# Output stage of a gated two-mixer decoder block: who adds, when the gates are multiplied, in what order the weights come

## The chip, the cores and the metric

The kernel runs on one core of a Trainium2 chip. The metric is the device time of one execution in microseconds (us). TensorE (PE) multiplies matrices into PSUM; VectorE (DVE), ScalarE (ACT) and GpSimd (POOL) work element by element; SyncE (SP) issues the DMAs.

## The reference, cut to what matters

One block on x of shape (1, 1024, 1024), all in float32:

```python
h = rmsnorm(x, mix_norm_g)
qa, ka, va, q_lat, kv_lat, k_r, g_a, g_b = split(h @ w_in)
o_a = sliding_window_attention(rope(qa), rope(ka), va, sinks)     # 8 heads of 64
o_b = latent_attention(q_lat, kv_lat, k_r)                        # 8 heads, causal
y = sigmoid(g_a) * (o_a @ w_o_swa) + sigmoid(g_b) * (o_b @ w_o_mla)
x = x + y @ w_out
h = rmsnorm(x, ffn_norm_g)
x = x + (silu(h @ w_gate) * (h @ w_up)) @ w_down
return rmsnorm(x, final_norm_g)
```

w_o_swa and w_o_mla are 512 x 1024, w_out is 1024 x 1024. The change lies in the line of y and in what leads up to it.

## The kernel before, in words

**Products.** Every float32 operand is split into a high part (a cast by ACT, L163) and a low part (a subtraction by DVE, L166); `split` (L161) does both. `mm3` (L168) makes one product out of three matmuls, high x high (L172), high x low (L173) and low x high (L174). Weights are loaded by `st.load_to` (the DMA is L238) into a raw tile `wr` and split by `st.conv_to`, in the order in which `plain` has listed them.

**Stages around the change.** First the projections and the sliding-window attention are done; o_a lies transposed in HBM (`oa_d`), the gates lie in HBM too (`gate_d`). Then comes the loop over the latent attention (L1353 to 1393): 64 tiles t = 8 heads x 8 blocks of 128 queries. One tile's turn issues the scores of tile t + 2 (L1171: matmuls L1182 to 1184 into `scb`, maximum on DVE, exp on ACT L1193, normalization on POOL), the pv products that have come due (L1213, matmuls L1231 and 1232 into `ob`), and the transposes of tile t (L1198: L1209 into `pTb`, split into `pth` and `ptl`).

**What is woven into the attention.** PE has the product o_a x w_o_swa as filling: `mix_a` (L1270) computes, for an output chunk dc of 128 columns and a half sh of 512 rows, 12 matmuls of 128x512 into `oA`, in halves of 6 at the tiles listed in `slots` (L1348), and copies the result with ACT (L1286) to `ar`; for dc below 4 that goes to HBM (`ar_d`) and comes back later. `units` (L1347) are the first 24 halves, `rest` (L1394) the four whole units left over. o_a itself is loaded by `load_oa` (L1249, tile `oar`) and split by `split_oa` (L1253). `load_q` and `load_k` fetch the next heads' queries and keys.

**The output stage** (L1400 to 1444): eight output chunks dc in the order `DCS` (L1304). For each, `load_sigs` (L1306) has fetched the two gates (tiles `sg`) and for dc below 4 `ar`; `sigmoids` (L1418) applies the sigmoid on ACT, a chunk ahead; `mix_b` (L1400) first lets POOL multiply `ar` with gate a (L1407, two halves), then for each half makes 12 matmuls o_b x w_o_mla into `oB` and lets DVE multiply the PSUM tile with gate b (L1412), then for each half adds the two (L1415 through `add`, L180: DVE for the first half, POOL for the second, except in the last chunk) and splits y into `yh` and `yl`, the operand of the next product. There are four PSUM banks for `oB` (psum_phase("psc", 4)). After the stage the product y x w_out runs (L1615, `xo`): for each block of 128 rows one sum over eight k = dc.

**What sets the order.** From L1039 to L1593 a scheduler orders the instructions of each engine out of the program by estimates; the order is not written out by hand. What runs through `tc.keep_in_program_order` (the casts of `split` while `held[0]` is set, L160 to 165) stays in its place. Each engine then runs its instructions in order. SP issues the DMAs in order too, and a DMA whose tile is not free holds up those behind it. Big tiles come from two pools of slots, U (21 of 128x1024) and V (17 of double size).

Of the kernel before, what the change touches and what calls it, by code (L numbers as in the profile page):

```python
# [89 lines left out]
def hybrid_block_kernel(  # L90
# [65 lines left out]
    def PX(name, shape=(P, 512)):  # L156
        return psum["x"].tile(list(shape), F32, tag="ps", name=uid(name))
# [10 lines left out]
    def mm3(ps, pairs, first=True, last=True, go_on=False):  # L168

        n = len(pairs)  # L170
        for i, ((ah, al), (bh, bl)) in enumerate(pairs):
            nc.tensor.matmul(ps, ah, bh, start=first and i == 0, stop=False, skip_group_check=go_on)  # L172
            nc.tensor.matmul(ps, ah, bl, start=False, stop=False, skip_group_check=go_on)  # L173
            nc.tensor.matmul(ps, al, bh, start=False, stop=last and i == n - 1, skip_group_check=go_on)  # L174
# [4 lines left out]
    def add(out, a, b, eng):  # L179
        eng.tensor_tensor(out, a, b, op=ALU.add)  # L180
# [4 lines left out]
    def half(s):  # L185
        return slice(512 * s, 512 * s + 512)
# [47 lines left out]
    def plain(key, src, shape, wide=False, k0=None):  # L234

        def load():
            raw = U("wr", F32, shape)
            nc.sync.dma_start(raw, src)  # L238
            return raw

        def conv(raw):
            hi, lo = halves_of(shape, wide)
            if k0 is None:
                split(hi, lo, raw)
            else:
                split_g(hi, lo, raw, k0)
            return hi, lo

        st.add(key, load, conv)
# [50 lines left out]
        plain(("oa", dp), w_o_swa[dp], (P, 4, 256), True)  # L300
    for dp in (2, 0, 3, 1):
        plain(("ob", dp), w_o_mla[dp], (P, 4, 256))
    for r, hf in enumerate((0, 1, 0)):
        for j in range(4):
            plain(("out", r, j), w_out[hf, j], (P, 2, 512), (r, j) != (2, 3))


# [945 lines left out]
    def split_oa(g, sh, c):  # L1253
        raw, (hi, lo) = oa_raw[(g, sh)] if c == 0 else oa_raw.pop((g, sh))
        split(hi[:, c], lo[:, c], raw[:, c])
        oaT[(2 * g + c, sh)] = (hi[:, c], lo[:, c])
# [5 lines left out]
        nc.sync.dma_start(gate[i], gate_d[i])  # L1262

    def sigmoid(i):
        nc.scalar.activation(gate[i], gate[i], AF.Sigmoid)

    ar = {}
    oa_ps = {}
# [25 lines left out]
    def split_ob(c, sh):  # L1294
        if sh == 0:
            ob_hl[c] = hi_lo("obT")
        hi, lo = ob_hl[c]
        src = ob.pop(c) if sh else ob[c]
        split(hi[:, half(sh)], lo[:, half(sh)], src[:, half(sh)])
        obT[(c, sh)] = (hi[:, half(sh)], lo[:, half(sh)])  # L1300

    wo = {}
    NT = NH * NB
    DCS = (4, 5, 0, 6, 1, 2, 3, 7)  # L1304

    def load_sigs(dc):  # L1306
        for i in (dc, 8 + dc):
            load_sig(i)
        if dc < 4:
            ar[dc] = U("ar")  # L1310
            nc.sync.dma_start(ar[dc], ar_d[dc])
# [32 lines left out]
    load_k(2)  # L1344
    first = {0: (2, 0), 1: (2, 1), 2: (3, 0), 3: (3, 1)}
    fill = {}
    units = [(u // 2, u % 2, c) for u in range(16 - 4) for c in (0, 2)]  # L1347
    slots = [5, 6] + [NB * h + n for h in range(1, NH) for n in (1, 2, 5)] + [NT - 2]  # L1348
    for t, u in zip(slots, units):
        fill[t] = u  # L1350
    w_at = {t: u[0] // 2 for t, u in fill.items() if u[0] % 2 == 0 and u[1:] == (0, 0)}
# [1 line left out]
    for t in range(NT):  # L1353
        h, n = divmod(t, NB)
        if t + 2 < NT:
            scores(t + 2)
        while pvq and pvq[0][0] <= t:
            pv(*pvq.pop(0)[1:])
        if n == 2 and h + 2 < NH:
            load_q(h + 2)  # L1360
        if n == 6 and h + 3 < NH:
            load_k(h + 3)
        hh, nn = step(t)
        if nn % 2 == 1:
            pvq.append((t + 3, hh, nn // 2))
        e = t - (NT - 8)
        if e == 6:
            psum_phase("psc", 4)
        if t in first:
            prod_k(*first[t])  # L1370
        if t in fill:
            dc, sh, c0 = fill[t]
            mix_a(dc, sh, c0, 2, P1("oA") if c0 == 0 else None)
        transposes(t)
        held[0] = True
        if t == 0:
            load_oa(0, 1)
            load_oa(1, 1)
        if t < 8:
            split_oa(t % 4 // 2, t // 4, t % 2)  # L1380
        if t + 6 in w_at or t == 0:
            st.load_to(st.index[("oa", w_at.get(t + 6, 0))])
        if t + 2 in w_at:
            st.conv_to(st.index[("oa", w_at[t + 2])])
        if e == 4:
            load_sigs(DCS[0])
        if -3 <= e < 3:
            split_ob((e + 3) // 2, (e + 3) % 2)
        if e in (2, 6):
            st.load_to(st.index[("ob", 2 if e == 2 else 0)])  # L1390
        if e == 6:
            st.conv_to(st.index[("ob", 2)])
        held[0] = False
    rest = [(i // 2, i % 2) for i in range(12, 16)]  # L1394
    mix_a(*rest.pop(0), 0, 4, PX("oA"))
    for _, hp, j in pvq:
        pv(hp, j)
# [2 lines left out]
    def mix_b(dc, i):  # L1400
        if dc % 2 == 0:
            wo[4 + dc // 2] = st.get(("ob", dc // 2))
        w = wo[4 + dc // 2]
        ga, gb = gate.pop(dc), gate.pop(8 + dc)
        a_ = ar.pop(dc)
        for sh in range(2):
            nc.gpsimd.tensor_tensor(ga[:, half(sh)], a_[:, half(sh)], ga[:, half(sh)], op=ALU.mult)  # L1407
        for sh in range(2):
            cs = half(sh)
            pb = PX("oB")  # L1410
            mm3(pb, [((w[0][:, c, blk(dc % 2)], w[1][:, c, blk(dc % 2)]), obT[(c, sh)]) for c in range(4)])
            nc.vector.tensor_tensor(gb[:, cs], pb, gb[:, cs], op=ALU.mult)  # L1412
        for sh in range(2):
            cs = half(sh)
            add(ga[:, cs], ga[:, cs], gb[:, cs], (nc.vector, nc.gpsimd)[sh * (i < 7)])  # L1415
            split(*hT(dc, cs), ga[:, cs])

    def sigmoids(dc):  # L1418
        for i in (dc, 8 + dc):
            sigmoid(i)  # L1420

    load_sigs(DCS[1])
    split_ob(3, 0)
    split_ob(3, 1)
    sigmoids(DCS[0])
    st.conv_to(st.index[("ob", 0)])
    new_quads("y")
    for i, dc in enumerate(DCS):
        if i in (0, 1):
            st.load_to(st.index[("ob", (3, 1)[i])])  # L1430
        if 3 <= i < 7:
            st.load_to(st.index[("out", 0, i - 3)])
        if i + 2 < 8:
            load_sigs(DCS[i + 2])
        if i + 1 < 8:
            sigmoids(DCS[i + 1])
        mix_b(dc, i)
        if rest:
            mix_a(*rest.pop(0), 0, 4, PX("oA"))
        if i in (1, 2):  # L1440
            st.conv_to(st.index[("ob", (3, 1)[i - 1])])
        if i >= 4:
            st.conv_to(st.index[("out", 0, i - 4)])
    st.conv_to(st.index[("out", 0, 3)])


    fg_bc = bcast_gain("ffng", ffn_g)
# [148 lines left out]
    for seg, (sh, hf) in enumerate(((0, 0), (0, 1), (1, 1), (1, 0))):  # L1596
        if seg == 3:
            in_order.__enter__()
        if seg in (0, 1, 3):
            r = {0: 0, 1: 1, 3: 2}[seg]  # L1600
            wo2 = [st.get(("out", r, j)) for j in range(4)]
        hs = half(hf)
        for b in range(4 * sh, 4 * sh + 4):
            if seg in (0, 2):
                x2[b] = load_x(b)
            if (seg, b) == (2, 4):
                ffn.load_part(0, 0)
            if (seg, b) == (2, 6):
                ffn.load_part(0, 1)
            if (seg, b) == (2, 7):  # L1610
                ffn.mix(0)
            if (seg, b) == (3, 6):
                ffn.prep_to(3)
            ps = P1("xo")
            mm3(ps, [(hT(k, blk(b)), (wo2[k // 2][0][:, k % 2], wo2[k // 2][1][:, k % 2])) for k in (0, 1, 4, 5, 2, 6, 3, 7)])  # L1615
            add(x2[b][:, hs], ps, x2[b][:, hs], nc.vector)
            if seg in (0, 2):
                st.conv_to(st.index[("out", seg // 2 + 1, b % 4)])
            if seg in (1, 3):
                xn = U("xn")  # L1620
                ss = tiny("ss")
                nc.scalar.activation(xn, x2[b], AF.Square, accum_out=ss)  # L1622
                rs = rstd_of(ss, D)
            lower = to_h(*prev) if prev is not None else None
            prev = None
            if seg in (1, 3):
                nc.vector.scalar_tensor_tensor(xn, x2[b], rs, fg_bc, op0=ALU.mult, op1=ALU.mult)
                prev = (xn, b)
                nc.sync.dma_start(x2_d[b], x2.pop(b))
            if (seg, b) == (3, 7):  # L1630
                for kh in range(2):
                    ffn.load_part(1, kh)
            if lower is not None:
                if seg == 3 and b >= 6:
                    late_parts.append(lower)
                else:
                    lower()
# [222 lines left out]
```

## Time and profile before

| | |
|---|---|
| time, median of 3 runs | 1360.06 us (1358.97 to 1360.89) |
| time of the profiled execution | 1360.02 us |
| its span, first to last instruction | 1357.8 us |
| PE, PEld busy | 1332.3, 1119.9 us |
| DVE, ACT, POOL busy | 896.7, 637.0, 577.2 us |
| mean granted clock of PE | 0.993 |
| HBM read, written | 151.72, 70.12 MB |

How to read it: the profile is one execution. A row of the timeline gives start, duration, engine, line, operation, the tile written and those read (buffer numbers left out), the shape, and in brackets the time for which the engine stood idle before it and who released it. Matmuls are pipelined, so one row's duration (0.39 us for 128x512) is longer than the distance of two starts. The windows give for a stretch its length, each engine's busy time with the number of its instructions, then the mean granted clock of PE (1.00 is full speed), the share of the DMA engines and GB/s. Groups give busy time, mean duration in ns, and the idle time just before them. In this kernel the attention loop with its filling runs from about 385 to 566 us, the output stage to 620 us, then the w_out product follows.

### The profile page before, as it was taken

What the parts mean: (1) busy time and instruction counts of PE and PEld (TensorE: products, weight loads), DVE (VectorE), ACT (ScalarE), POOL (GpSimd) and SP (SyncE); (2) the same over time, 40 slices, a digit from 0 to 9 for tenths busy, and PEclk for the clock granted to TensorE, in tenths of its full rate; (3) what the DMA queues carried; (4) which work ended last, traced back from release to release, by engine and by line L of the source; (5) the groups of instructions that cost most, each with busy time, mean ns of one, the idle gap of its engine ahead of it and who ended that gap; (6) DMA issues with size and microseconds to landing.
All of it is one profiled execution on the core that took longest, in us unless ns stands there. A gap on an engine that the chain in (4) does not pass through costs nothing.

```text
span 1357.8 us, 19019 instructions
## 1 busy us (share of the span) xinstructions
PE 1332.3 (98%) x6564; PEld 1119.9 (82%) x6564; DVE 896.7 (66%) x1462; ACT 637.0 (47%) x1293; POOL 577.2 (43%) x621
## 2 busy tenths in 40 slices
PE   9999999999999999998999999999999999999997
PEld 6899878878878888786887888888888888888886
DVE  7868767776767667665458866666656654664862
ACT  7434666675446776753336232322332332644443
POOL 2126546452224555462031465766665551022521
PEclk9999999999998999999999999999999999999999
DMA  9454322335575430671343353645435425997504
GB/s 371 151 190 160 117 89 79 121 109 190 162 256 139 105 89 33 232 263 63 110 170 133 127 178 139 230 179 178 148 140 178 163 85 181 379 367 258 171 10 146
DMA packets 85311, 223.61 MB, mean 165 GB/s; under 512 B 9632, under 2 KB 16288, under 8 KB 84128
## 3 DMA queue, kind: packets, MB, share of 16 engines
q1 hardware_dynamic: 83776, 220.05, 47.1%
q10 hardware_dynamic: 1440, 2.36, 0.5%
q8 instruction: 52, 0.85, 0.3%
q14 instruction: 43, 0.35, 0.1%
HBM read 151.72 MB, written 70.12 MB: 163 GB/s over the span
## 4 chain that ended last, share of the span: by engine, by line
PE 79%; POOL 6%; issue 5%; DVE 5%; ACT 4%; DMA 1%; POOLq 0%; ACTq 0%; DVEq 0%
PE fa L174 7%; PE fa L172 7%; PE fa L173 7%; PE fb L174 6%; PE fb L172 6%; PE fb L173 6%; PE fd L174 5%; PE fd L172 5%; PE fd L173 5%; POOL p L1195 2%; POOL denb L1194 2%; PE xo L172 2%; PE xo L174 2%; PE xo L173 2%; POOL sg L180 1%
## 5 line engine op out<-in xcount | busy, mean ns | idle before, releaser
L166 DVE TENSOR_TENSOR wl<-wr,wl 128x512 fp32r<-128x512 f32 x150 | 149.9, 1023 | 72.4 <-ACT wl L163 72.0
L166 DVE TENSOR_TENSOR lrv<-lr,lrv 128x1024 fp32r<-128x1024 f32 x77 | 105.0, 1397 | 49.1 <-ACT lrv L163 44.9
L163 ACT CAST lrv<-lr 128x1024 fp32r<-128x1024 f32 x77 | 80.1, 1052 | 95.7 <-PE fd L174 53.7
L172 PE MATMUL fd<-lrv 128*128 128x512 f32 x308 | 119.8, 389 | 0.0
L173 PE MATMUL fd<-lrv 128*128 128x512 f32 x308 | 119.8, 389 | 0.0
L174 PE MATMUL fd<-lrv 128*128 128x512 f32 x308 | 119.8, 389 | 0.0
L177 POOL TENSOR_TENSOR wr<-wr,sm 128x512 f32<-128x512 f32 (+1 forms) x38 | 46.4, 1229 | 149.1 <-DVE wl L166 116.9
L163 ACT CAST wl<-wr 128x512 fp32r<-128x512 f32 x150 | 86.9, 623 | 1.9 <-DVE wr L831 1.6
L1194 POOL TENSOR_TENSOR denb<-denb,neg_one 128x1 f32<-128x1 f32 x64 | 38.5, 601 | 98.5 <-ACT p L1193 94.1
L166 DVE TENSOR_TENSOR wl<-sm,wl 128x512 fp32r<-128x512 f32 x60 | 49.2, 847 | 45.8 <-ACT wl L163 45.7
L310 POOL TENSOR_SCALAR ms<-ss 128x1 f32<-128x1 f32 x32 | 8.8, 274 | 144.0 <-ACT xn L1622 67.6
L173 PEld LDWEIGHTS fd<-lrv 128*128 128x128 f32 x308 | 57.8, 188 | 12.1
L174 PEld LDWEIGHTS fd<-lrv 128*128 128x128 f32 x308 | 57.8, 188 | 12.0
L172 PEld LDWEIGHTS fd<-lrv 128*128 128x128 f32 x308 | 57.8, 188 | 11.9
L1193 ACT ACTIVATE p<-scb,nmb 128x384 f32<-128x384 f32 (+3 forms) x64 | 47.8, 746 | 35.5 <-DVE nmb L1192 31.5
L166 DVE TENSOR_TENSOR ptl<-pTb,pth 128x512 fp32r<-128x512 f32 (+2 forms) x96 | 50.6, 553 | 16.5 <-ACT pth L163 15.9
L1192 DVE CUSTOM_DVE_ANT_0 scb<-scb,mask 128x384 f32<-128x384 f32 (+3 forms) x64 | 48.6, 762 | 16.2 <-PE scb L1184 14.2
L1514 ACT ACTIVATE act<-sm 128x512 f32<-128x512 f32 x11 | 7.0, 633 | 105.2 <-DVE sm L180 105.2
L172 PE MATMUL xo<-wv,yh 128*128 128x512 f32 x120 | 48.1, 401 | 3.2 <-ACT yh L163 3.2
L1195 POOL TENSOR_SCALAR p<-p,denb 128x384 f32<-128x384 f32 (+3 forms) x64 | 47.8, 747 | 6.3
L163 ACT CAST pth<-pTb 128x512 fp32r<-128x512 f32 (+2 forms) x96 | 43.3, 484 | 9.2 <-PE pTb L1209 8.6
L174 PE MATMUL xo<-wv,yl 128*128 128x512 f32 x120 | 47.5, 396 | 0.0
(356 smaller groups left out, 4298.8 us busy)
## 6 DMA issues: line engine op xcount, KB each, us to landing
lr<-la_d SPq DMA_DIRECT2D x77, 256.0 KB, 5.4
wr<-in_w_gate_dram SPq DMA_DIRECT2D x22, 512.0 KB, 4.3
wr<-in_w_up_dram SPq DMA_DIRECT2D x22, 512.0 KB, 5.2
wd<-in_w_down_dram SPq DMA_DIRECT2D x22, 512.0 KB, 6.6
rb_d<-wd SPq DMA_DIRECT2D x22, 512.0 KB, 2.7
la_d<-sd SPq DMA_DIRECT2D x22, 512.0 KB, 4.8
lr<-rb_d SPq DMA_DIRECT2D x44, 256.0 KB, 5.4
lr<-in_w_down_dram SPq DMA_DIRECT2D x33, 256.0 KB, 5.6
```

The costliest lines, as they stand in the source:

```text
L163: i = nc.scalar.copy(hi, src)
L166: (eng or nc.vector).tensor_tensor(lo, src, hi.bitcast(F32), op=ALU.subtract)
L172: nc.tensor.matmul(ps, ah, bh, start=first and i == 0, stop=False, skip_group_check=go_on)
L173: nc.tensor.matmul(ps, ah, bl, start=False, stop=False, skip_group_check=go_on)
L174: nc.tensor.matmul(ps, al, bh, start=False, stop=last and i == n - 1, skip_group_check=go_on)
L177: eng.tensor_tensor(out, a, b, op=ALU.subtract)
L180: eng.tensor_tensor(out, a, b, op=ALU.add)
L310: nc.gpsimd.tensor_scalar(ms, ss, 1.0 / width, EPS, op0=ALU.mult, op1=ALU.add)
L1192: nc.vector.tensor_tensor_reduce(s_, s_, m_, 1.0, -NEG, op0=ALU.add, op1=ALU.min, accum_out=nm)
L1193: nc.scalar.activation(p_, s_, AF.Exp, scale=-1.0, bias=nm, accum_out=den)
L1194: nc.gpsimd.tensor_tensor(den, den, neg_one[:, 0:1], op=ALU.pow)
L1195: nc.gpsimd.tensor_scalar(p[:, 0:w], p[:, 0:w], den, 0.0, op0=ALU.mult, op1=ALU.add)
```

## The change

It has five parts.

1. In `mix_b` all additions (L1415) are issued on DVE; before, seven of 16 were on POOL.
2. POOL's gate products (L1407) move from `mix_b` into `sigmoids`, so that they are issued a chunk ahead.
3. `DCS` becomes (4, 5, 0, 1, 6, 7, 2, 3), chunks that share a weight tile one after the other. The loads of w_o_mla and w_out and their conversions are issued at other steps, w_out's first round in the order (2, 0, 3, 1), and the sum in `xo` takes k in the order of `DCS`.
4. The first chunk's sigmoids are held in program order, behind the splits of the last o_b chunk.
5. In the attention loop 26 halves of the w_o_swa product instead of 24 are placed (a fourth slot in heads 1, 3 and 5, none at the last but one tile), and the three units left over instead of four are issued ahead of each chunk's o_b products instead of behind; `load_q` is issued at n == 4 instead of 2, `load_oa` of the second row half at t == 3 instead of 0, and its splits at t = 6 to 9 instead of 4 to 7.

In the order in which the engines issue, DVE has seven additions more and POOL seven fewer; PE has the same matmuls, with the last oA units all ahead of the first oB; ACT has the table load and the first sigmoid behind the last casts of `obT` instead of behind the copy to `otb`; and SP has the first load of w_o_swa ahead of the two `oar` loads of the second row half instead of behind them.

```diff
+    OUT0 = (2, 0, 3, 1)
     for r, hf in enumerate((0, 1, 0)):
-        for j in range(4):
+        for j in (range(4) if r else OUT0):
             plain(("out", r, j), w_out[hf, j], (P, 2, 512), (r, j) != (2, 3))
...
     def sigmoid(i):
-        nc.scalar.activation(gate[i], gate[i], AF.Sigmoid)
+        a = nc.scalar.activation(gate[i], gate[i], AF.Sigmoid)
+        if held[0]:
+            tc.keep_in_program_order(a)
...
-    DCS = (4, 5, 0, 6, 1, 2, 3, 7)
+    DCS = (4, 5, 0, 1, 6, 7, 2, 3)
...
-    units = [(u // 2, u % 2, c) for u in range(16 - 4) for c in (0, 2)]
-    slots = [5, 6] + [NB * h + n for h in range(1, NH) for n in (1, 2, 5)] + [NT - 2]
+    units = [(u // 2, u % 2, c) for u in range(16 - 3) for c in (0, 2)]
+    slots = [5, 6] + [NB * h + n for h in range(1, NH) for n in (1, 2, 5, 6) if n < 6 or h in (1, 3, 5)]
...
-        if n == 2 and h + 2 < NH:
+        if n == 4 and h + 2 < NH:
             load_q(h + 2)
...
-        if t == 0:
+        if t == 3:
             load_oa(0, 1)
             load_oa(1, 1)
-        if t < 8:
-            split_oa(t % 4 // 2, t // 4, t % 2)
+        if t < 4 or 6 <= t < 10:
+            split_oa(t % 4 // 2 if t < 4 else (t - 6) // 2, t // 6, t % 2)
...
-    rest = [(i // 2, i % 2) for i in range(12, 16)]
+    rest = [(i // 2, i % 2) for i in range(13, 16)]
...
-        a_ = ar.pop(dc)
-        for sh in range(2):
-            nc.gpsimd.tensor_tensor(ga[:, half(sh)], a_[:, half(sh)], ga[:, half(sh)], op=ALU.mult)
...
-            add(ga[:, cs], ga[:, cs], gb[:, cs], (nc.vector, nc.gpsimd)[sh * (i < 7)])
+            add(ga[:, cs], ga[:, cs], gb[:, cs], nc.vector)
             split(*hT(dc, cs), ga[:, cs])
 
     def sigmoids(dc):
         for i in (dc, 8 + dc):
             sigmoid(i)
+        a_ = ar.pop(dc)
+        for sh in range(2):
+            nc.gpsimd.tensor_tensor(gate[dc][:, half(sh)], a_[:, half(sh)], gate[dc][:, half(sh)], op=ALU.mult)
 
     load_sigs(DCS[1])
     split_ob(3, 0)
     split_ob(3, 1)
+    held[0] = True
     sigmoids(DCS[0])
+    held[0] = False
     st.conv_to(st.index[("ob", 0)])
     new_quads("y")
     for i, dc in enumerate(DCS):
-        if i in (0, 1):
-            st.load_to(st.index[("ob", (3, 1)[i])])
-        if 3 <= i < 7:
-            st.load_to(st.index[("out", 0, i - 3)])
+        if i in (1, 2):
+            st.load_to(st.index[("ob", (3, 1)[i - 1])])
+        if 2 <= i < 6:
+            st.load_to(st.index[("out", 0, OUT0[i - 2])])
         if i + 2 < 8:
             load_sigs(DCS[i + 2])
+        if rest:
+            mix_a(*rest.pop(0), 0, 4, PX("oA"))
         if i + 1 < 8:
             sigmoids(DCS[i + 1])
         mix_b(dc, i)
-        if rest:
-            mix_a(*rest.pop(0), 0, 4, PX("oA"))
-        if i in (1, 2):
-            st.conv_to(st.index[("ob", (3, 1)[i - 1])])
+        if i in (2, 3):
+            st.conv_to(st.index[("ob", (3, 1)[i - 2])])
         if i >= 4:
-            st.conv_to(st.index[("out", 0, i - 4)])
-    st.conv_to(st.index[("out", 0, 3)])
+            st.conv_to(st.index[("out", 0, OUT0[i - 4])])
...
-            mm3(ps, [... for k in (0, 1, 4, 5, 2, 6, 3, 7)])
+            mm3(ps, [... for k in DCS])
```

More of the change, by code (lines that the diff above doesn't have):

```diff
@@ L1614, in hybrid_block_kernel @@
             ps = P1("xo")
-            mm3(ps, [(hT(k, blk(b)), (wo2[k // 2][0][:, k % 2], wo2[k // 2][1][:, k % 2])) for k in (0, 1, 4, 5, 2, 6, 3, 7)])
+            mm3(ps, [(hT(k, blk(b)), (wo2[k // 2][0][:, k % 2], wo2[k // 2][1][:, k % 2])) for k in DCS])
             add(x2[b][:, hs], ps, x2[b][:, hs], nc.vector)
```

## The prediction, written before the result

> **What bounds the kernel now.** I read the busy shares of the page first, then the granted clock, then the table of windows over the stretches that the change touches, and last the timelines of PE, ACT, SP and DVE at the places where PE stands still.
>
> ```profile
> PE 1332.3 (98%) x6564; PEld 1119.9 (82%) x6564; DVE 896.7 (66%) x1462; ACT 637.0 (47%) x1293; POOL 577.2 (43%) x621
> core 0: 1357.8 us, clock 0.993
> ```
>
> TensorE is busy for 98% of the span at almost full clock, and the change takes no matmul away: PE issues the same products in another order. So it can only win what PE loses between its matmuls, or what it loses to a lower clock after them. The windows show where that is (columns: PE, PEld, DVE, ACT, POOL busy, granted clock, DMA share, GB/s).
>
> ```profile
> 404.00:408.20 4.20, 0.56 (x5) 0.36 (x3) 0.33 (x2) 1.04 (x1) 0.00 (x0) 0.89 1.03 276
> 408.20:414.20 6.00, 6.00 (x21) 5.30 (x22) 3.48 (x7) 3.24 (x8) 2.67 (x4) 0.51 1.06 317
> 556.00:560.00 4.00, 1.99 (x14) 1.43 (x13) 1.22 (x4) 3.96 (x7) 2.02 (x3) 1.00 0.93 333
> 560.00:566.00 6.00, 5.97 (x25) 4.98 (x26) 3.32 (x5) 2.82 (x4) 0.52 (x1) 0.72 0.91 307
> 566.00:620.00 54.00, 52.63 (x233) 43.01 (x232) 35.16 (x39) 31.27 (x40) 31.89 (x20) 1.00 0.72 258
> 620.00:628.30 8.30, 5.10 (x24) 3.90 (x22) 5.38 (x9) 4.01 (x7) 1.84 (x1) 1.00 0.00 0
> 628.30:633.00 4.70, 4.70 (x13) 3.41 (x14) 3.98 (x6) 2.37 (x3) 0.00 (x0) 0.64 0.00 0
> ```
>
> Three holes stand out (404, 556 and 620 us), and behind each the clock falls for some microseconds although PE is then fully busy. What a lowered clock costs is length x (1 - clock): 6.00 x 0.49 = 2.94 us, 6.00 x 0.28 = 1.68 us, 4.70 x 0.36 = 1.69 us. Each hole thus costs its wait and this tail.
>
> **Step 1: the first w_o_swa weights (load order, slots in the first head).** Timelines of SP, ACT and PE around 404 us:
>
> ```profile
> 396.44 1.48 SPq L1251 DMA_DIRECT2D oar<-oa_d  x2
> 398.01 0.45 SPq L238 DMA_DIRECT2D wr<-in_w_o_swa_dram  x1
> 402.54 0.68 ACT L163 CAST wv<-oar 128x512 fp32r<-128x512 f32 x1
> 407.05 1.04 ACT L163 CAST wv<-wr 128x1024 fp32r<-128x1024 f32 x1 [3.83 <-DMA wr<-in_w_o_swa_dram]
> 404.23 0.28 PE L1184 MATMUL scb<-kT,qT 96*128 96x256 f32 x1
> 408.14 0.79 PE L172 MATMUL oA<-wv,wv 128*128 128x512 f32 x1 [3.64 <-ACT wv L163]
> ```
>
> The landings of the same DMAs, from the DMA issues of 395 to 409 us:
>
> ```profile
> oar<-oa_d SPq DMA_DIRECT2D x2, 512.0 KB, 6.4
> wr<-in_w_o_swa_dram SPq DMA_DIRECT2D x1, 512.0 KB, 9.0
> ```
>
> The weight load is issued behind two oar loads of 512 KB each, lands at 398.0 + 9.0 = 407.0, and is what ACT and then PE wait for. From the last score matmul (404.23) to the first oA (408.14) pass 3.91 us where 0.13 would do: 3.78 lost, plus 2.94 of clock, **6.7 us**. In the changed kernel these two oar loads, load_oa(0, 1) and (1, 1), are issued at t = 3, and the weight load takes the first one's place in SP's queue, at about 396.4. With that one's landing time, 6.4, it is there at 402.8; ACT is done with the cast before it at 402.54 + 0.68 = 403.2. So the cast isn't late any more, and PE has further scores and pv products ahead of oA in the new order. What is late next: the moved oar loads, two DMA issues on SP past the weights. They are first split at t = 6 instead of 4, three tiles after their issue, and their products start in slot 9, three tiles after the first split; I cost this at nothing, and at 1 us (a guess between nothing and the 2.94 above) if that cover is gone. The later load_q (n == 4) feeds scores some ten tiles on; at nothing as well.
>
> **Step 2: the first sigmoids.** ACT and PE at the tail of the attention:
>
> ```profile
> 555.59 1.28 ACT L1265 ACT_TABLE_LOAD   x1
> 556.89 1.06 ACT L1265 ACTIVATE sg<-sg 128x1024 f32<-128x1024 f32 x1
> 557.97 0.59 ACT L1286 COPY ar<-oA 128x512 f32<-128x512 f32 x1
> 558.45 1.25 ACT L163 CAST pth<-pTb 128x512 fp32r<-128x512 f32 x3
> 558.61 0.44 PE L1209 MATMUL pTb<-ident,p 128*128 128x128 f32 x2 [1.23 <-ACT ar L1286]
> 559.82 0.39 PE L1231 MATMUL ob<-pth,vM 128*128 128x256 f32 x1 [0.77 <-DVE ptl L166]
> ```
>
> The table load and one sigmoid (2.3 us) stand on ACT ahead of the copy that frees a PSUM bank and of the casts that the last pv needs. PE waits 1.23 and 0.77; each gap also loses the overlap of two matmuls (0.39 shown, 0.23 between starts in the rows of step 3, so 0.16 each): 2.32, and with 1.68 of clock **4.0 us**. Held in program order they come behind both obT casts. There PE has the oA products that now stand ahead of all oB (a whole unit is 24 matmuls, 5.5 us) and the first oB half (2.8 us), while ACT needs 1.28 + 2 x 1.06 = 3.4 us until DVE's first multiplication. Hidden; without that cover it would cost up to 3.4 us. The three rest units instead of four only move 12-matmul halves into heads 1, 3 and 5, at equal PE time.
>
> **Step 3: the output stage.** PE's matmuls at its pitch and at its three waits, and the others' rows:
>
> ```profile
> 612.23 0.39 PE L173 MATMUL oB<-obT,wh 128*128 128x512 f32 x1
> 612.46 0.39 PE L174 MATMUL oB<-obT,wl 128*128 128x512 f32 x1
> 613.30 0.50 PE L172 MATMUL oB<-obT,wh 128*128 128x512 f32 x1 [0.46 <-DVE sg L1412]
> 617.22 0.50 PE L172 MATMUL oB<-obT,wh 128*128 128x512 f32 x1 [0.91 <-DVE sg L1412]
> 628.20 0.50 PE L172 MATMUL xo<-wv,yh 128*128 128x512 f32 x1 [3.20 <-ACT yh L163]
> 612.56 0.68 DVE L1412 TENSOR_TENSOR sg<-oB,sg 128x512 f32<-128x512 f32 x1
> 613.28 1.58 DVE L180 TENSOR_TENSOR sg<-sg,sg 128x512 f32<-128x512 f32 x1
> 615.55 1.02 DVE L166 TENSOR_TENSOR yl<-sg,yh 128x512 fp32r<-128x512 f32 x1 [0.69 <-ACT yh L163]
> 617.31 2.13 POOL L180 TENSOR_TENSOR sg<-sg,sg 128x512 f32<-128x512 f32 x1 [1.30 <-DVE sg L1412]
> 620.13 0.69 DVE L166 TENSOR_TENSOR yl<-sg,yh 128x512 fp32r<-128x512 f32 x1 [1.83 <-ACT yh L163]
> 620.74 0.69 DVE L1412 TENSOR_TENSOR sg<-oB,sg 128x512 f32<-128x512 f32 x1
> 621.46 0.69 DVE L180 TENSOR_TENSOR sg<-sg,sg 128x512 f32<-128x512 f32 x1
> ```
>
> PE loses 0.46 + 0.91 + 3.20 = 4.57, with 0.16 of overlap and some 0.1 of slow first matmul for each of three gaps 5.35, and 1.69 of clock: **7.0 us**. Why: DVE runs in order, and a yl split in it waits for ACT's cast, which waits for POOL's addition (2.13 us). DVE stands for 1.83 us, then starts the next multiplication, and PE's banks come free late: from 612.56 to 620.74 one tile of 24 matmuls takes DVE 8.2 us, PE needs 24 x 0.23 = 5.5.
>
> The changed stage, by groups of the window 566 to 629 us:
>
> ```profile
> L166 DVE TENSOR_TENSOR yl<-sg,yh 128x512 fp32r<-128x512 f32 x15 | 12.8, 852 | 17.3 <-ACT yh L163 17.1
> L1412 DVE TENSOR_TENSOR sg<-oB,sg 128x512 f32<-128x512 f32 x16 | 10.9, 683 | 1.6 <-PE oB L174 1.6
> L180 DVE TENSOR_TENSOR sg<-sg,sg 128x512 f32<-128x512 f32 x8 | 9.2, 1152 | 0.3
> L166 DVE TENSOR_TENSOR wv<-wr,wv 128x1024 fp32r<-128x1024 f32 x4 | 4.8, 1212 | 0.0
> L1407 POOL TENSOR_TENSOR sg<-ar,sg 128x512 f32<-128x512 f32 x14 | 21.4, 1546 | 17.4 <-ACT sg L1265 17.4
> ```
>
> Seven additions go from POOL to DVE; DVE then does per half a multiplication, an addition, a split and 7/16 of a weight conversion (0.53), and its own addition now feeds the cast, after which it waits about 0.7 (the 0.69 above) where nothing stands between; the new order shows that at some five halves of 16, so 0.2 per half. How long the additions take beside POOL's products the trace shows only for before's mix, so I bound the time of one half p. From above: the group means, 0.68 + 1.15 + 0.85 + 0.53 + 0.2, less 0.09 overlap of three (0.69 shown, 0.60 between starts) = 3.15 us. From below: all at the 0.69 of the rows of 620 and 621 us, where POOL is idle, 0.60 x 3 + 0.5 + 0.2 = 2.5 us. PE's half is 12 x 0.23 = 2.76. DVE starts when the first half ends; the last tile's first half of y is needed 21 matmuls (4.8 us) after the last oB, as the xo sum takes that tile last. So y is late by 2.76 + 15p + 0.6 - (16 x 2.76 + 4.8) = 15p - 45.6: zero at p = 3.04. I take p = 2.8, between the ends, because POOL's seven additions (2.13 each) are gone, and with its 14 products alone it is busy for 21.4 of some 44 us instead of the 31.9 of 54 in the window that made the means. Then xo doesn't wait. Products a tile ahead take them off the chain from the sigmoids to the addition; sigmoid, product and load of the next tile have about one tile (5.5 us) of room, against 2 x 1.06 + 2 x 1.55 = 5.2 us of work that starts a tile earlier than before: at nothing, otherwise the addition waits and counts in p. The pair order and the ob and out loads leave the counts as they are; the last weight conversions stand in DVE's queue behind the earlier tiles, at nothing beyond the 0.53.
>
> A rule of the Trainium skill ("GPSIMD Engine Reference", section "8. Key points") speaks against the additions on DVE: POOL shares its SBUF interfaces with VectorE and collides with DVE instructions of two SBUF inputs. The trace agrees: the addition at 613.28 took 1.58 us, the one at 621.46 0.69. By that rule the upper end of p holds, which is the first rival.
>
> **Sum.** 6.7 + 4.0 + 7.0 = 17.7 us. I leave 0.7 for small new waits, estimated from the 0.46 and 0.91 above as half of one pair, since DVE lags PE in some halves. Profiled execution: span 1357.8, time 1360.02 (2.2 around it), against the runs' median of 1360.06, so no correction: 1360.0 - 17.0 = **1343 us**.
>
> The clock part has a rule of its own in the Trainium skill ("TensorE: Matmul & The Clock Gate", section "Why this matters for your kernels"): no idle gaps above about 3 us, or the clock drops to half. The waits of 3.64 and 3.20 agree; the waits of 1.23 and 0.77 were followed by a clock of 0.72 all the same, so the measurement decides. By the rule alone step 2 would give 2.3 instead of 4.0, and the sum would be 1.7 smaller.
>
> **Rivals.**
> - **DVE becomes the bound of the output stage** (p from 3.1 to 3.3). For it: means of 1.15 and 0.85 us beside POOL. Against: less POOL work. At 3.15 xo waits 1.6 and the clock costs 1.7 again, at 3.3 it is 3.9 + 1.7: 1342.3 + 3.3 to 5.6, about 1346 to 1348.
> - **One of the first two holes stays**: the weight load lands at its 9.0 us again (396.4 + 9.0 = 405.4, 2.2 us after ACT is free, with clock up to 5), or the held sigmoids delay the first oB by 3.4. Against: the load issued first lands sooner (6.4 against 9.0). About 1347 to 1350.
> - **Slower**: the additions on DVE collide with POOL's products in every half and each yh is waited for: 0.68 + 1.58 + 0.69 + 1.02 + 0.53 = 4.5 us per half, so y is 21.9 late, mostly as waits for PSUM banks, plus 1.7 of clock; less the 17.7, 6 us slower, 1366. It decides from 15p - 45.6 + 1.7 = 17.7, p = 4.1. For it: the rows of 612 to 616. Against: POOL is busy half of the time at most, and DVE's 8.2 us per tile (4.1 per half) contain POOL's additions.
> - **The change doesn't do what it says**: the order of the instructions shows it does for loads, sigmoids, additions and products, so this has no share of its own; partly eaten gains (p near 4.0) end within 0.2%.
>
> **How the numbers follow.** Forecast (1341 to 1345) 0.60; DVE bound 0.18; a hole that stays 0.10; within 0.2% of before (2.7 us, about what a measurement of this kernel can tell from no change) 0.05; slower 0.07. Faster is 0.60 + 0.18 + 0.10 = 0.88. The range takes in the first three cases and 1 us for the lower end (the small oA waits nearby): 1340 to 1351, leaving out about 0.15.
>
> **What would show it.** Right: no wait above 1 us for wv at the first oA, for pTb at the tail or for yh at the first xo; clock 1.00 in those stretches; DVE a tile in about 5.5 us. Wrong: the first w_o_swa cast waits for its DMA; PE waits for sg at L1412's line in a row of halves; additions on DVE with a mean above 1.3 us; a new wait in heads 0 and 1 for the moved oar loads.

## The result and the profile after

The changed kernel takes 1346.54 us (median of 4 runs, 1346.08 to 1348.25), against 1359.51 us of the kernel before beside it (4 runs, 1355.64 to 1360.89): a ratio of 0.9911, 95% interval 0.9889 to 0.9934, so 9 to 15 us less. The profiled execution took 1346.17 us with a span of 1344.4; before it was 1360.02 and 1357.8.

The page's row of busy times, then the windows over the stretches shown for before (the output stage now ends earlier, so its windows are cut anew):

```profile
PE 1326.3 (99%) x6564; PEld 1114.7 (83%) x6564; DVE 903.8 (67%) x1469; ACT 636.8 (47%) x1293; POOL 567.7 (42%) x614
```

```profile
404.00:408.20 4.20, 4.20 (x29) 3.71 (x28) 3.85 (x8) 2.78 (x6) 2.06 (x2) 1.00 1.01 341
408.20:414.20 6.00, 6.00 (x38) 4.97 (x36) 3.75 (x9) 4.73 (x13) 2.59 (x4) 1.00 1.05 261
556.00:560.00 4.00, 4.00 (x27) 3.60 (x26) 2.25 (x3) 2.32 (x4) 0.00 (x0) 1.00 1.01 368
560.00:566.00 6.00, 6.00 (x30) 5.03 (x29) 1.98 (x3) 4.71 (x7) 0.58 (x1) 1.00 0.98 367
566.00:600.00 34.00, 34.00 (x150) 27.89 (x150) 28.23 (x33) 23.00 (x29) 17.75 (x12) 1.00 0.80 290
600.00:608.00 8.00, 8.00 (x37) 6.62 (x36) 8.00 (x11) 5.13 (x7) 4.43 (x3) 1.00 0.99 371
608.00:616.00 8.00, 6.81 (x31) 5.32 (x29) 7.72 (x11) 2.68 (x5) 3.10 (x2) 1.00 0.04 16
616.00:626.00 10.00, 10.00 (x44) 7.99 (x43) 5.18 (x7) 4.02 (x5) 0.00 (x0) 1.00 0.00 0
```

PE is busy through 404 to 408 (4.20 of 4.20, before 0.56) and through 556 to 560 (4.00 of 4.00, before 1.99), and the clock stays at 1.00 in every one of these windows. One hole is left, 1.19 us between 608 and 616. Between 600 and 616 DVE is busy for 8.00 of 8.00 and 7.72 of 8.00 us: that is the new limit. The rows of PE's timeline show the hole, as a wait for yh, and three small new waits in the attention ahead of it:

```profile
414.83 0.51 PE L1183 MATMUL scb<-kT,qT 96*128 96x512 f32 x1 [0.63 <-ACT p L1194]
422.15 0.50 PE L173 MATMUL oA<-wv,wv 128*128 128x512 f32 x1 [0.51 <-DVE wv L166]
...
555.23 0.66 PE L1210 MATMUL pTb<-ident,p 128*128 128x128 f32 x4 [0.78 <-POOL p L1196]
...
615.65 0.50 PE L172 MATMUL xo<-wv,yh 128*128 128x512 f32 x1 [1.19 <-ACT yh L163]
```

ACT's cast of the first w_o_swa weights (the second row), for which PE stood still at 404, no longer waits: it has no bracket.

```profile
403.13 0.64 ACT L163 CAST wv<-oar 128x512 fp32r<-128x512 f32 x1
403.65 1.07 ACT L163 CAST wv<-wr 128x1024 fp32r<-128x1024 f32 x1
```

**A measure for what follows.** All kernels here have the same matmuls in the same order up to about 398 us, and still their profiled executions differ there by some us. So each profile is also read by PE's lost time: from each matmul's start to the next, less the median distance that matmuls of its shape have in the kernel before, summed over a stretch. It contains waits and low clock. In us, from the profiled executions:

| kernel | to 396 | 396 to 535 (hole 404) | 535 to 569 (hole 558) | 569 to 634 (hole 620) | behind 634 | from 396 on |
|---|---|---|---|---|---|---|
| before | 13.5 | 10.3 | 5.9 | 7.2 | 1.8 | 25.3 |
| changed | 13.5 | 5.3 | 2.2 | 1.8 | 2.6 | 11.8 |
| e1 first head | 19.1 | 5.5 | 4.4 | 6.9 | 1.8 | 18.6 |
| e2 hold | 15.9 | 10.1 | 2.5 | 7.9 | 1.8 | 22.4 |
| e3 additions | 13.3 | 8.9 | 5.6 | -0.1 | 1.8 | 16.2 |
| e4 stage | 15.7 | 8.1 | 4.3 | 0.4 | 2.2 | 15.0 |
| f1 POOL adds | 13.9 | 5.1 | 2.4 | 8.9 | 2.7 | 19.1 |
| f2 no products | 14.8 | 5.1 | 2.4 | -0.1 | 1.8 | 9.2 |
| f4 oar early | 14.5 | 4.1 | 2.2 | 1.6 | 2.2 | 10.1 |
| g1 oA behind | 15.1 | 5.2 | 2.4 | 2.2 | 2.5 | 12.3 |
| g2 four units | 15.4 | 5.5 | 2.5 | 1.4 | 1.9 | 11.3 |
| h1 no hold | 14.0 | 5.1 | 2.7 | 2.9 | 2.5 | 13.2 |
| i1 not ahead | 15.0 | 5.1 | 2.4 | 1.9 | 2.6 | 12.0 |
| k1 three edits | 16.2 | 4.3 | 2.6 | 0.5 | 1.8 | 9.3 |

From before to the changed kernel the three holes' stretches lose 5.1, 3.7 and 5.4 us less and the rest 0.8 more; together that is 13.4, as much as the spans differ by. Where the clock stays up the measure repeats to 0.3 us (the changed kernel and i1, which has the same order, as shown below). Where the clock falls behind a hole it does not: ahead of 535 us before, e2, e3 and e4 do PE's work in the same order, and lose 10.3, 10.1, 8.9 and 8.1 between 396 and 535.

### The profile page after: what moved, and what is told of

It is laid out like the page before. It is cut to its first block, busy times and chain, and to the rows that moved or that the text cites. A ratio compares the mean times of both kernels' runs of the same rounds, so it can differ in the third digit from the quotient of the medians.

```text
span 1344.4 us, 19030 instructions
## 1 busy us (share of the span) xinstructions
PE 1326.3 (99%) x6564; PEld 1114.7 (83%) x6564; DVE 903.8 (67%) x1469; ACT 636.8 (47%) x1293; POOL 567.7 (42%) x614
## 4 chain that ended last, share of the span: by engine, by line
PE 50%; DVE 2%; ACT 1%; issue 1%; POOL 1%; DMA 0%; SPq 0%; POOLq 0%; ACTq 0%; DVEq 0%
PE fa L174 6%; PE fa L172 6%; PE fa L173 6%; PE fd L173 5%; PE fd L174 5%; PE fd L172 5%; PE fb L172 4%; PE fb L174 4%; PE fb L173 4%; PE xo L174 2%; PE xo L172 2%; PE xo L173 2%; DVE lrv L166 0%; DMA lr<-in_w_down_dram 0%; PE tp L1464 0%
## 5 line engine op out<-in xcount | busy, mean ns | idle before, releaser
L166 DVE TENSOR_TENSOR wl<-wr,wl 128x512 fp32r<-128x512 f32 x150 | 152.7, 1042 | 72.2 <-ACT wl L163 71.9
L166 DVE TENSOR_TENSOR wl<-sm,wl 128x512 fp32r<-128x512 f32 x60 | 48.9, 841 | 45.7 <-ACT wl L163 45.6
L172 PE MATMUL fb<-t2h,wl 128*128 128x512 f32 x120 | 47.4, 395 | 0.0
```

The lines of the kernel that those rows point to most:

```text
L166: (eng or nc.vector).tensor_tensor(lo, src, hi.bitcast(F32), op=ALU.subtract)
```

## The experiments

The times, each against the kernel before run beside it:

| kernel | median us | before us | ratio, 95% interval |
|---|---|---|---|
| e1 | 1354.73 | 1357.59 | 0.9979 [0.9967, 0.9990] |
| e2 | 1358.19 | 1357.59 | 1.0001 [0.9989, 1.0012] |
| e3 | 1350.56 | 1357.59 | 0.9950 [0.9935, 0.9965] |
| e4 | 1352.23 | 1357.59 | 0.9963 [0.9950, 0.9976] |
| f2 | 1344.99 | 1360.44 | 0.9892 [0.9868, 0.9917] |
| g1 | 1346.88 | 1360.44 | 0.9906 [0.9885, 0.9928] |
| g2 | 1346.58 | 1360.44 | 0.9904 [0.9883, 0.9925] |
| f4 | 1345.26 | 1360.44 | 0.9894 [0.9874, 0.9915] |
| h1 | 1348.98 | 1359.32 | 0.9926 [0.9911, 0.9941] |
| f1 | 1353.89 | 1359.32 | 0.9960 [0.9945, 0.9975] |
| i1 | 1347.06 | 1359.32 | 0.9911 [0.9896, 0.9926] |
| k1 | 1344.45 | 1359.32 | 0.9890 [0.9873, 0.9906] |

### One part of the change put into the kernel before

**e1, the first head alone.**

```diff
-        if n == 2 and h + 2 < NH:
+        if n == 4 and h + 2 < NH:
             load_q(h + 2)
-        if t == 0:
+        if t == 3:
             load_oa(0, 1)
             load_oa(1, 1)
-        if t < 8:
-            split_oa(t % 4 // 2, t // 4, t % 2)
+        if t < 4 or 6 <= t < 10:
+            split_oa(t % 4 // 2 if t < 4 else (t - 6) // 2, t // 6, t % 2)
```

> The kernel before with one part: load_oa(0, 1) and (1, 1) at t == 3, their splits at t = 6 to 9, load_q at n == 4. Theory (the holes are independent, each part fills its own): the wait of 3.64 us at the first oA and the low clock behind it go, 6.2 us less in the stretch 404 to 416; the two new small waits that the changed kernel shows at 414.8 (0.80) and 422.2 (0.68) come along, so about 4.7 to 5.2 us less in all, near 1355. Rival (the time comes back later, the holes at 558 and 620 grow): 2 us less or nothing.

The hole at 404 is gone, and the stretch 396 to 535 loses 4.8 us less, as expected. e1 moves three things; of these k1 below has only the two loads, moved by one tile, and the hole is gone too. So the place of these two loads in SP's queue, ahead of the first weights, made it. The time fell by 2.9 us only (1.4 to 4.5). The profiled execution, the slowest of its ten, lost 5.7 us more ahead of 396, in code that is not touched; how much of that the other runs have is not known. And the hole at 558 shows something that was not expected: the same two waits as before, 1.23 and 0.77 us, this time without a low clock. Windows of e1 and then of before:

```profile
560.00:563.00 3.00, 2.29 (x15) 1.99 (x16) 2.95 (x5) 3.00 (x6) 1.40 (x2) 1.00 0.74 246
```

```profile
560.00:563.00 3.00, 2.97 (x14) 2.57 (x15) 2.95 (x5) 2.82 (x4) 0.52 (x1) 0.65 0.81 228
```

The clock column reads 1.00 against 0.65. Behind the same waits it fell in e3 (0.70), and in e4 it did not (1.00). So the fall behind a hole of this size comes in some executions and not in others, and is no fixed part of its price.

**e2, the hold alone.**

```diff
-        nc.scalar.activation(gate[i], gate[i], AF.Sigmoid)
+        a = nc.scalar.activation(gate[i], gate[i], AF.Sigmoid)
+        if held[0]:
+            tc.keep_in_program_order(a)
...
+    held[0] = True
     sigmoids(DCS[0])
+    held[0] = False
```

> The kernel before with one part: the first chunk's sigmoids held in program order behind the last obT splits. Theory: the waits of 1.23 and 0.77 us go and with them the low clock behind them, about 4.3 us less, near 1355.5. Rival 1: the low clock doesn't hang on waits that short, so only some 2.3 us less. Rival 2: the sigmoids come late for the first gate multiplication and the output stage starts up to 3.4 us later: no gain.

The waits at 558 shrink to one of 0.69 us and the stretch loses 3.4 us less; the output stage loses 0.7 more, PE waiting for sg up to 1.56 us. The time is unchanged (1.0001, about 1.5 us either way). None of the three expectations holds whole: the hole went as the theory said, and the time did not follow, as rival 2 said, but the stage lost 0.7 us and not 3.4. Two things stand against the gain. In the profile 2.5 us more are lost ahead of 396. And the mean clock of e2's ten runs is 0.994 or 0.995, that of the 20 runs of before 0.996 in the mean; as an estimate, 0.001 of 1358 us is 1.4 us. How much of the gain either hides in the other runs is open.

**e3, the additions alone.**

```diff
-            add(ga[:, cs], ga[:, cs], gb[:, cs], (nc.vector, nc.gpsimd)[sh * (i < 7)])
+            add(ga[:, cs], ga[:, cs], gb[:, cs], nc.vector)
```

> The kernel before with one part: all additions of L1415 on DVE. Theory (the chain multiplication, POOL addition of 2.13 us, cast, split sets the stage, and DVE's stand of 1.83 us goes with it): the xo wait of 3.20 us falls to some 1 us and the clock stays up, 4 to 5.5 us less, near 1355. Rival (the additions beside POOL's products take 1.3 to 1.6 us on DVE and eat the gain): 0 to 2 us less, or slower.

More than expected: 7.0 us less (4.8 to 8.8). PE has no wait of 0.3 us or more left between 569 and 634 (lost time -0.1, before 7.2). This one line is worth about half of the whole change.

**e4, the whole stage without the rest**: the changed kernel with heads, units and sigmoids of the kernel before. The diff shows the units; `rest`, the moved loads and splits and the hold are taken back as well.

```diff
-    units = [(u // 2, u % 2, c) for u in range(16 - 3) for c in (0, 2)]
-    slots = [5, 6] + [NB * h + n for h in range(1, NH) for n in (1, 2, 5, 6) if n < 6 or h in (1, 3, 5)]
+    units = [(u // 2, u % 2, c) for u in range(16 - 4) for c in (0, 2)]
+    slots = [5, 6] + [NB * h + n for h in range(1, NH) for n in (1, 2, 5)] + [NT - 2]
```

> The changed kernel with its output stage (additions on DVE, products a chunk ahead, chunk order, load order, oA ahead of oB) but with the heads, the slots and the sigmoids of the kernel before (four rest units). Theory: the stretch 566 to 633 loses 5.4 us as in the changed kernel, the holes at 404 and 558 stay: near 1354. Rival (the stage's gain needs the shorter tail ahead of it, because unheld sigmoids with products behind them delay the obT casts): 3 us less or under, with a larger hole near 558.

The stage loses 6.8 us less than before, with the additions alone it was 7.3. So the other parts of the stage, chunk order and load order among them, add nothing to the additions. The gain doesn't hang on the shorter tail either: the rival falls.

### One part taken out of the changed kernel, or turned

**f1, additions on POOL again.**

```diff
-            add(ga[:, cs], ga[:, cs], gb[:, cs], nc.vector)
+            add(ga[:, cs], ga[:, cs], gb[:, cs], (nc.vector, nc.gpsimd)[sh * (i < 7)])
```

> The changed kernel with seven of the additions on POOL again. Theory (the additions alone fill the hole at 620): PE waits for sg and for yh again, 5 us or more in the stage, near 1352. Rival (products a chunk ahead and the chunk order fill it too): 0 to 2 us more.

The hole comes back, with waits for sg and for yh, on PE's timeline of f1:

```profile
607.79 0.50 PE L172 MATMUL oB<-obT,wh 128*128 128x512 f32 x1 [1.55 <-DVE sg L1412]
...
621.60 0.50 PE L172 MATMUL xo<-wv,yh 128*128 128x512 f32 x1 [3.31 <-ACT yh L163]
```

Lost time is 8.9 in the stage against 1.8, and the time about 7 us longer. Together with e3: for this hole the additions are needed, and they suffice.

**i1, products back in mix_b.**

```diff
+        a_ = ar.pop(dc)
+        for sh in range(2):
+            nc.gpsimd.tensor_tensor(ga[:, half(sh)], a_[:, half(sh)], ga[:, half(sh)], op=ALU.mult)
...
-        a_ = ar.pop(dc)
-        for sh in range(2):
-            nc.gpsimd.tensor_tensor(gate[dc][:, half(sh)], a_[:, half(sh)], gate[dc][:, half(sh)], op=ALU.mult)
```

> The changed kernel with POOL's gate products back in mix_b, not a chunk ahead. Theory (POOL is idle for most of the stage, so the products come in time either way): within 0.7 us of the changed kernel's 1346.5, the xo wait between 0.7 and 2. Rival (the additions on DVE then wait for POOL): 2 to 4 us more, with waits on DVE for POOL.

The same time, and the same wait of 1.19 us at xo to the hundredth. The reason is plainer than the theory: in the two traces every engine has the same instructions in the same order (buffer numbers left out), POOL's products too. The scheduler places them alike in both programs. So the second part of the change does nothing, and i1 is no test of products that come earlier; it is the changed kernel measured a second time.

**f2, no gate products.** The kernel leaves the first mixer's product out of y, so its result is not the block's; it serves to time DVE without POOL beside it.

```diff
-        a_ = ar.pop(dc)
-        for sh in range(2):
-            nc.gpsimd.tensor_tensor(gate[dc][:, half(sh)], a_[:, half(sh)], gate[dc][:, half(sh)], op=ALU.mult)
+        ar.pop(dc)
```

> The changed kernel without POOL's gate products of the output stage: the factor of the first mixer's product, ar, is left out of y, all else is computed. It measures what POOL's 14 to 16 products cost DVE. Theory (collision with POOL makes DVE the bound at the end of the stage): DVE's additions fall from a mean of 0.925 to 0.69 us, the yl splits from 0.844 to 0.69, and the wait of 1.19 us at xo goes, with its slow start 1.8 us less: near 1344.7 against 1346.5 of the changed kernel. Rival (the waits for yh and the order of DVE's work set the end, not the collision): durations fall, but the xo wait stays above 0.8 us.

DVE's groups between 564 and 618 us (busy, mean ns | idle before), first of the changed kernel, then of f2:

```profile
L180 DVE TENSOR_TENSOR sg<-sg,sg 128x512 f32<-128x512 f32 x16 | 14.6, 925 | 0.6
L166 DVE TENSOR_TENSOR yl<-sg,yh 128x512 fp32r<-128x512 f32 x16 | 13.4, 844 | 4.2 <-ACT yh L163 3.9
L1412 DVE TENSOR_TENSOR sg<-oB,sg 128x512 f32<-128x512 f32 x16 | 10.9, 679 | 0.0
L166 DVE TENSOR_TENSOR wv<-wr,wv 128x1024 fp32r<-128x1024 f32 x4 | 5.9, 1465 | 0.0
```

```profile
L1412 DVE TENSOR_TENSOR sg<-oB,sg 128x512 f32<-128x512 f32 x16 | 11.0, 686 | 2.2 <-PE oB L174 2.1
L166 DVE TENSOR_TENSOR yl<-sg,yh 128x512 fp32r<-128x512 f32 x16 | 10.8, 687 | 4.0 <-ACT yh L163 3.9
L180 DVE TENSOR_TENSOR sg<-sg,sg 128x512 f32<-128x512 f32 x16 | 10.7, 687 | 0.3
L166 DVE TENSOR_TENSOR wv<-wr,wv 128x1024 fp32r<-128x1024 f32 x5 | 6.1, 1216 | 0.0
```

Without POOL beside it DVE's additions fall from 925 to 687 ns, the splits from 844 to 687, the weight splits from 1465 to 1216. The multiplication, which takes one operand from PSUM, stays (679, 686). DVE now waits for PE (2.1 us), the xo wait is gone, and the time is 1.5 us lower. That the additions had waited for the products is no rival: they stood idle for 0.6 us in all, and for 0.3 in f2. So without the collision with POOL the last hole isn't there. The Trainium skill ("GPSIMD Engine Reference", section "8. Key points") states this contention, for DVE instructions with two SBUF inputs. The trace agrees, and puts 0.24 us on an addition as the mean over this stage.

**h1, sigmoids not held.**

```diff
-    held[0] = True
     sigmoids(DCS[0])
-    held[0] = False
```

> The changed kernel with the first chunk's sigmoids not held. Theory (the hold fills the hole at 558, but shifts the first gate products on POOL into DVE's additions, which costs the xo wait): the waits of 1.4 and 0.9 us at 558 come back, with or without a low clock (0 to 1.7), and the xo wait of 1.35 goes with its slow start: 0.6 to 2.4 us more than the changed kernel's 1346.5. Rival (the hold costs nothing later): 2.3 to 4 us more and the xo wait unchanged.

The theory fell. The hole at 558 did not come back (2.7 against 2.2). Without the hold the sigmoid stands ahead of pth casts again, but nothing that PE needs at once stands behind it. Before, that was the copy to ar of the unit that ended at tile 62, for whose bank pTb waited, and the slot at tile 62 is gone. PE runs oA matmuls between its pv products meanwhile. So either of two parts fills that hole: e2 and g2 have the hold with the old slots, h1 the new slots without the hold, and e4, which has neither, keeps it (4.3). What the hold buys in the changed kernel lies in the stage. PE's timeline and a DVE group of h1:

```profile
617.59 0.50 PE L172 MATMUL xo<-wv,yh 128*128 128x512 f32 x1 [2.47 <-ACT yh L163]
```

```profile
L180 DVE TENSOR_TENSOR sg<-sg,sg 128x512 f32<-128x512 f32 x15 | 16.5, 1108 | 0.5
```

The additions take 1108 ns instead of 925, and the xo wait is 2.47 instead of 1.19: when the sigmoids move, the products move, and more of them meet an addition. That this is the cause is argued from f2, not shown by itself.

**g1, one oA unit behind the first chunk; g2, four units left over as before.** g1 moves two lines of the loop, g2 takes back the two lines shown as a diff for e4 (and `rest`).

```diff
-        if rest:
-            mix_a(*rest.pop(0), 0, 4, PX("oA"))
         if i + 1 < 8:
             sigmoids(DCS[i + 1])
         mix_b(dc, i)
+        if rest:
+            mix_a(*rest.pop(0), 0, 4, PX("oA"))
```

> The changed kernel with the last of the three left-over oA units behind the first chunk's oB products instead of ahead of them. Theory (DVE works without a pause from its first multiplication at 569.0 to the end, and that start is set by the held sigmoids and a weight split ahead of it, not by PE): no change, the xo wait stays at 1.0 to 1.4 us, near 1346.5. Rival (PE's first oB sets DVE's start; 2.7 us earlier): the xo wait goes, 1.8 us less.

> The changed kernel with the units and slots of the kernel before: 24 halves in the heads, one at the last but one tile, four units left over, one of them behind the first chunk. Theory (the xo wait is DVE's lag in a stage that is one unit, 2.7 us of PE, shorter; the new wait of 0.87 us for POOL at 555 comes from the slot taken from the last but one tile): both go, 1.8 + 1.0 us less, near 1343.7. Rival (the wait hangs on DVE's time for a half alone): xo wait as in the changed kernel, only the 1.0 of the tail is won.

Both keep the time. In g1 the xo wait fell to 0.60 us, and a wait for a weight split took its place (rows of g1):

```profile
590.75 0.50 PE L174 MATMUL oB<-obT,wl 128*128 128x512 f32 x1 [0.81 <-DVE wl L166]
617.71 0.51 PE L172 MATMUL xo<-wv,yh 128*128 128x512 f32 x1 [0.60 <-ACT yh L163]
```

In g2 the wait for POOL at 555 became one for ptl, and the xo wait is still 0.91 (rows of g2):

```profile
555.36 0.39 PE L1232 MATMUL ob<-pth,vM 128*128 128x256 f32 x1 [0.69 <-DVE ptl L166]
617.69 0.50 PE L172 MATMUL xo<-wv,yh 128*128 128x512 f32 x1 [0.91 <-ACT yh L163]
```

My theory for g2 fell, that for g1 held for the time only. One unit of 2.7 us between the first chunks, which gives DVE that much more time, is not enough here; in g2 the additions take 1059 ns. e4, with the same unit there and the sigmoids not held, has no such wait. Its first multiplication starts 2.92 us after the first oB matmul, in g2 4.45.

**f4, oar loads and splits earlier.**

```diff
-        if t == 3:
+        if t == 1:
             load_oa(0, 1)
             load_oa(1, 1)
-        if t < 4 or 6 <= t < 10:
-            split_oa(t % 4 // 2 if t < 4 else (t - 6) // 2, t // 6, t % 2)
+        if t < 8:
+            split_oa(t % 4 // 2, t // 4, t % 2)
```

> The changed kernel with load_oa(0, 1) and (1, 1) at t == 1 and their splits at t = 4 to 7 as before; the first weight load stays ahead of them. Theory (the two new small waits at 414.8 and 422.2, 0.80 and 0.68 us from start to start, come from the splits moved to t = 6 to 9, where ACT and DVE have the second head's work): the second goes, the first falls to some 0.5, about 1 us less, near 1345.5, and no hole at 404. Rival (the splits now wait for their loads): a wait on ACT for oar, no gain or 1 us more.

The wait of 422 is gone and that of 414.8 is down to 0.20 us, but a new one stands earlier (row of f4):

```profile
400.37 0.51 PE L172 MATMUL k<-ckv,wv 128*128 128x512 f32 x1 [0.58 <-DVE kns L166]
```

Lost time from 396 to 535 is 4.1 against 5.3, and counted from 398 us PE reaches the same point of the same work 1.2 us earlier. The time is 1.3 us lower than the changed kernel's, and 1.3 and 1.6 lower than that of g2 and g1, run beside it. So the theory held in its size: the later splits cost about 1.2 us.

**k1, three edits of the kernel before**: e3's line, e2's hold, and

```diff
-        if t == 0:
+        if t == 1:
             load_oa(0, 1)
             load_oa(1, 1)
```

> The kernel before with three edits: all additions on DVE, load_oa(0, 1) and (1, 1) at t == 1 instead of 0, first sigmoids held. Products, chunk order, slots, units and splits as before. Theory (these three fill the three holes, the other parts buy nothing): as fast as the changed kernel or up to 2 us faster, 1344.5 to 1346.5. Rival (the holes need the other parts, the hold costs the stage as much as it wins without them): 1348 or more.

1344.45 us, ratio 0.9890 [0.9873, 0.9906]. i1 ran beside it and has the changed kernel's order: it took 1346.48 to 1347.88 us, k1 1343.69 to 1346.42, so every run of k1 is faster than every run of i1, by 2.6 us in the medians. In the profiles k1 loses 2.5 us less than the changed kernel from 396 on. So these three edits do all that the change does, and its other parts cost time: 0.9 us in the first head, 1.3 in the output stage and 0.7 behind 634, against 0.5 won at 558. PE has no wait of 0.3 us in the stage, with two oA units between its oB products (windows of k1, then its group of additions on DVE):

```profile
566.00:600.00 34.00, 34.00 (x152) 28.15 (x151) 30.99 (x34) 23.82 (x30) 19.75 (x13) 1.00 0.66 236
600.00:614.00 14.00, 14.00 (x64) 11.58 (x63) 12.70 (x16) 6.38 (x9) 5.88 (x4) 1.00 0.72 288
614.00:634.00 20.00, 19.95 (x87) 15.91 (x86) 9.75 (x13) 5.58 (x7) 0.00 (x0) 1.00 0.00 1
```

```profile
L180 DVE TENSOR_TENSOR sg<-sg,sg 128x512 f32<-128x512 f32 x16 | 18.2, 1138 | 0.9 <-DVE sg L1414 0.5
```

How the three share the gain is less certain than the sum. The medians of e1, e2 and e3 differ from before by 2.9, -0.6 and 7.0 us, 9.3 in all, and k1's by 14.9. In the profiles the stretches where each acts lose 4.8, 3.4 less 0.7, and 7.3 us less, 14.8 in all, and k1 loses 16.0 less; the 1.2 between them is what f4 finds for the moved splits, which e1 has and k1 has not.

## Why the prediction was right, and where it was off

Faster was right, and the range 1340 to 1351 holds 1346.5. The likeliest case (1341 to 1345) is not what came: the first rival is, "DVE becomes the bound of the output stage", whose 1346 to 1348 holds the measured time. The forecast took off 17.0 us; the profiled spans differ by 13.4. Of the 3.6 missing, step 1 lacks 1.6, step 2 0.3, step 3 0.9, and 0.8 is lost behind 634, where nothing was costed (one wait of 0.37 us at 1144 is part of it; the rest was not followed up).

**Step 1**, 6.7 us. The mechanism was right: moving the two loads alone fills the hole (k1), and the cast starts at 403.65, against the forecast 403.2. The stretch gained 5.1. Mis-sized was "I cost this at nothing, and at 1 us": the moved splits left new waits (0.63 and 0.51 at 414.8 and 422.2), and f4, with the splits back in their place, is 1.2 us faster there. The second of the two values was the right one.

**Step 2**, 4.0 us. The stretch gained 3.7. The hole went, but not only by the cause named: h1 lacks the hold and has no such hole. "The three rest units ... only move 12-matmul halves" was wrong: the move filled it too, and where it is made a wait of 0.78 for POOL stands at 555. The 1.68 of clock in this step was no fixed price, as e1 and e4 show; the 3.7 contains it because before's profile happens to be one with this fall, which is luck for the number. Two slips: a half is 6 matmuls, not 12, and a unit 12 (2.7 us), not 24; two units stood there, so the 5.5 us of cover were right.

**Step 3**, 7.0 less 0.7. The stage gained 5.4. The step that failed is "I take p = 2.8, between the ends". DVE's first multiplication starts at 569.02 and the fifteenth half's split ends at 616.32 (its rows on DVE's timeline):

```profile
569.02 0.68 DVE L1412 TENSOR_TENSOR sg<-oB,sg 128x512 f32<-128x512 f32 x1
...
615.63 0.69 DVE L166 TENSOR_TENSOR yl<-sg,yh 128x512 fp32r<-128x512 f32 x1
```

(616.32 - 569.02 - 0.6) / 15 = 3.11 us per half; counted to the start of xo at 615.65 it is 3.07. Both are close to the upper end 3.15. The forecast drew p down because POOL would be busy for 21.4 of some 44 us. POOL was busy for 25.3 of 50 (the three windows from 566 to 616), about that share, but it did not bring the durations down as far: the additions fell from 1152 to 925 ns, the splits stayed at 844 (852 before), and four of the seven weight splits rose to 1465, where the sum had 1212. f2 shows what POOL adds: without it additions and splits take 687. (The seven additions on POOL, "2.13 each" in the forecast, had taken 1.79 in the mean, 12.6 us in all.)

By the prediction's own formula 15 x 3.11 - 45.6 = 1.05 us late; measured 1.19. That the two are so close is partly luck, because DVE began 3.21 us after the first oB matmul (565.81) and not 2.76. Of the prediction's own signs two failed with it: the wait for yh is above 1 us, and DVE takes some 6.2 us for a tile (twice 3.11), not 5.5. The rival had 1.7 of clock with it, and the clock stayed at 1.00.

Of the other costs at nothing, chunk and load order held (e4). The products a chunk ahead were not put to the test, as their order did not change (i1). Not weighed at all was that oA ahead of oB takes from DVE the time that such units give it when they stand between: e3 and k1 keep two of them there and show no wait, k1 with additions of 1138 ns. That this order is the reason is argued; no run changes it alone.

## What to carry to other kernels

Read the bound engine from start to start of its work, and not only by its idle column, and do it stretch by stretch. What a hole costs, and what is left when it is filled, can be seen there even when executions differ elsewhere by more than an edit is worth.

An engine that runs in order and waits for a slower one's result in the middle of a chain pays for the whole chain. So giving it that step itself can be cheaper although its busy time grows (e3: DVE waited 1.83 us for additions of 2.13 on POOL). When work moves onto an engine, price it at what the row costs beside its neighbour, and do the same for the work that is there already.

Take a change of many parts apart. Here three small edits do more than all five parts together, and one part did not even change the order of the instructions.

## What the runs showed of the hardware

The granted clock behind a short hole is not settled by the hole: the waits of 1.23 and 0.77 us at 558 were followed by 0.65 and 0.70 (before, e3) and by 1.00 (e1, e4). Single waits of 2.38 (e4) and 2.92 us (e3) at 404 were followed by 0.54 and 0.70, one of 2.47 at 617 (h1) by 1.00. Behind waits of 3.2 us and more the clock fell in every profile here that has one (0.51 in before at 408, 0.64 at 628; so too in e1, e2 and f1). The other runs of before have mean clocks of 0.993 to 0.998. As an estimate, a run at 0.998 can have lost no more than about 2.7 us to the clock in its whole span (0.002 of 1358), so not every run of before paid the 6.3 us of clock that the prediction counted. The Trainium skill ("TensorE: Matmul & The Clock Gate", section "What's actually happening") says that the window which decides runs freely, so the same kernel can fare differently. The rows at 558 agree with that, but no run shows the window itself.

An addition of two SBUF tiles of 128x512 on DVE took 687 ns with POOL silent and 925 to 1138 in the mean beside POOL's products (changed, k1); with one operand in PSUM it took 686 and 679 (f2, changed). And the stretch ahead of 396 us, the same code in all kernels, lost between 13.3 and 19.1 us.
